# The head of a two-layer backbone: first two chunks modulated one at a time, squares of x summed by TensorE, x ahead of ctx

## The chip, the core and the metric

The kernel runs on one core of one Trainium2 chip. The metric is device time in microseconds (us) of one execution; lower is better. PE is TensorE (matrix products), ACT is ScalarE, DVE is VectorE, SP is SyncE, which here issues all large transfers.

## What is computed

Two layers work on 256 latent tokens (x) and 256 context tokens (ctx) of 2048 channels each. The change lies at the start of layer 0, in the modulated norm and the first part of the input projection:

```
shift_x, scale_x, gate_x = split(silu(c) @ ada_w[0] + ada_b[0], 3)
shift_c, scale_c, gate_c = split(silu(c_ctx) @ ada_w[0] + ada_b[0], 3)
hx = rmsnorm(x, norm_w[0]) * (1 + scale_x) + shift_x
hc = rmsnorm(ctx, norm_w[0]) * (1 + scale_c) + shift_c
q, k, v, ga, u, gb = split(hx @ w_in)        # and the same of hc
```

Everything else (retention, Fourier mixing, gates, output projections, the convolution layer, the final norm) follows it and is written the same in both kernels.

## The kernel before

Channels lie on the 128 partitions and tokens on the free axis. x comes in four tiles xT of 4 channel chunks each (a chunk is 128 channels by 256 tokens, 512 KB a tile), ctx in four tiles cT. Products are made in parts: a weight tile is split into a high part whi (ACT, L95) and the rest wlo (DVE, L59), an activation into a high and a low half of its tile, and three products are summed in PSUM. Products of plain fp32 operands (the sums of squares, gemv) go over PE in two records each.

The head is a sequence of eighths e = 0..7 of 256 channels (two chunks) each.

* `norm_sums` squares the four tiles on ACT (L237, L240; tiles nacc and sq), adds them on DVE (L65), sums over the partitions with two products by a matrix of ones on PE (into pvx for x, pvc for ctx), and takes the root (ACT, L245) and the reciprocal (DVE, L246): rs_x, rs_c.
* `load_ada(e)` loads four tiles (1 MB each) of the modulation weights of one eighth, scale and shift columns of 256 channels. `gemv` multiplies each by the silu of the two conditioning vectors (sc): four products of 512 columns, which use 32 columns of PE each, so four run side by side. `gather` copies the result out of PSUM (gs, L270), `modulation` turns rows into columns with four small products by a selector (gemv<-cols,gs, called row products below) and adds bias and weight on DVE (md), and `mod_stream` makes two modulated chunks of x or of ctx: a DVE step (modt, L196), an ACT step that writes the high half (hx or hc, L197), and a DVE step that writes the low half (L198).
* `main_k` and `main_v` are the dense products of a chunk: q and k of two heads (banks pk and pq), v in pvx, and for ctx k (pk) and v (pvc), with one weight tile w0s[e] per eighth.

In the loop over e the gemv work of eighth e+2 is done between the dense products of eighth e. After eighth 7 ACT makes the silu of a broadcast copy of c (scb) and copies pk, pvx and pvc out of PSUM; then come the projections with streamed weight tiles (gT, gN, gD).

Buffers set who waits: `raw` has 3 slots, which weight tiles w0s and the tiles 0 and 2 of load_ada share in turn; tiles 1 and 3 have a slot each (tags v and scb); whi and wlo have 6. All transfers go through SP in one order. The source fixes which work there is; a scheduler of the language then decides the order of the instructions on each engine, from its own costs, so a change in one place can move rows elsewhere.

```
mds = [prepare(0, load_ada(0))]
mod_stream(0, mds[0], 0)
wraw = load_raw(a["w0s"][0])
load_x(cT, a["ctxT"])
norm_sums(cT, rs_c, pvc[:, 0, :])
mod_stream(0, mds[0], 1)
mds.append(prepare(1, load_ada(1)))
mod_stream(1, mds[1], 0)
mod_stream(1, mds[1], 1)
wn = split_w(wraw, spare)
```

Of the kernel before, what the change touches and what calls it, by code (L numbers as in the profile page):

```python
"""Two-layer hybrid retention / Fourier / short-convolution backbone with a context prefix.

Everything runs in channel-major form (channels on partitions, tokens on the free axis), so
modulation, gates, norms' weights and the convolution are per-partition scalars, and no
activation is ever transposed.  Matrix products are carried by float32r passes: each operand is
split exactly into two 12-bit parts (x = hi + lo) and hi*hi + lo*hi + hi*lo is accumulated in PSUM.
"""
# [13 lines left out]
D = 2048  # L21
# [6 lines left out]
# columns of the packed per-channel vectors  # L28
C_C, C_CC, C_AB0, C_NW0, C_ABG, C_NW1, C_FNW, C_LOG, C_CV, C_SEL = 0, 16, 32, 64, 80, 144, 160, 176, 192, 288
N_COLS = 290  # L30
# columns of the packed shape-only tables
# [4 lines left out]
def body(tc, a, out):  # L36
    nc = tc.nc
    es = ExitStack()
    with es:
# [27 lines left out]
        # ---------------------------------------------------------------- constants  # L67
# [11 lines left out]
        # ---------------------------------------------------------------- weight stream  # L79
# [5 lines left out]
        def split_w(raw, spare=None):  # L85
            """Exact 12-bit parts of a weight tile, by quarters; the last quarter can use spare slots."""
            parts = []
            for pc in range(4):
                sl = raw[:, pc * 512:(pc + 1) * 512]
                if spare and pc == 3:  # L90
                    hi, lo = spare()
                else:
                    hi = wp.tile([P, 512], F32R, tag="whi", bufs=6, name="whi")
                    lo = wp.tile([P, 512], F32R, tag="wlo", bufs=6, name="wlo")
                nc.scalar.copy(hi[:], sl)  # L95
                sub(lo[:], sl, hi[:])
                parts.append((hi, lo))
            return parts
# [6 lines left out]
        def bg():  # L105
            """One background task at every second weight tile."""
            if quiet[0]:
                return
            turn[0] ^= 1
            if tasks and turn[0]:  # L110
                tasks.pop(0)()
# [7 lines left out]
        def group_t(wd, i0, nkt, streams):  # L119
            """Channel-major product of 256 output columns; per stream a pair of banks [hi.W + lo.hi | lo.W]."""  # L120
            ps = [psum("gT") for _ in streams]
            for kt in range(nkt):
                raw = load_raw(wd[i0 + kt])
                bg()
                for pc, (hi, lo) in enumerate(split_w(raw)):
                    for k2 in range(2):
                        kc = kt * 8 + pc * 2 + k2
                        fst, lst = kc == 0, kc == nkt * 8 - 1
                        for t, st in zip(ps, streams):
                            x = st[kc // 2]  # L130
                            for m in range(2):
                                c0 = k2 * 256 + m * 128
                                mm(t[:, m, :], hi[:, c0:c0 + 128], x[:, kc % 2, :], fst, False)
                                mm(t[:, m, 0:256], lo[:, c0:c0 + 128], x[:, kc % 2, 0:256], False, lst)
                    if pc % 2:
                        hook()
            return ps

        def group_d(wd, i0, nkt, x):
            """As group_t for one stream, with all three products summed in place: a bank of two column halves."""  # L140
# [16 lines left out]
        def group_n(wd, i0, streams):  # L157
            """Token-major product of 512 output columns; per stream a pair of banks (token tiles)."""
# [19 lines left out]
        def lr(pool, t, name="t2", bufs=5):  # L178
            """Sum of the two halves of a channel-major bank pair."""
            r = pool.tile([P, 2, 256], F32, tag="t2", bufs=5, name="lr_r")  # L180
            nc.scalar.copy(r[:], t[:, :, 256:512])
            s = pool.tile([P, 2, 256], F32, tag=name, bufs=bufs, name=name)
            add(s[:], t[:, :, 0:256], r[:])
            return s

        def rstd_bc(pool, ps_sum, n):
            """Reciprocal root of the mean plus eps, from sums already broadcast over partitions."""
# [5 lines left out]
        def modulate(pool, dst, x, col, shift, rs):  # L193
            """dst (hi | lo) = x * col * rs + shift."""
# [6 lines left out]
        def split_act(dst, y):  # L201
            """dst[:, m] = (hi | lo) of y[:, m]."""
# [9 lines left out]
        # ---------------------------------------------------------------- start: norms and first modulation  # L212
# [34 lines left out]

        scol = const.tile([P, 32], F32, name="scol")
# [3 lines left out]
        # 1 + scale bias  # L252
# [7 lines left out]
        norm_sums(xT, rs_x, pvx[:, 0, :])  # L260
# [6 lines left out]
        def gather():  # L267
            """Copies the four partial rows out of PSUM."""
# [4 lines left out]
        def modulation(e, gs):  # L273
            """Rows to columns; (scale, shift) of both streams, then the modulated chunks of this eighth."""
# [18 lines left out]
        def main_k(e, k2, w):  # L293
            hi, lo = w
            kc = 2 * e + k2
            for x, blocks in ((hx[e], kq_x), (hc[e], k_c)):
# [7 lines left out]
        def main_v(e, k2, w):  # L304
            hi, lo = w
            kc = 2 * e + k2
            for x, t in ((hx[e], pvx), (hc[e], pvc)):
# [17 lines left out]
        mds = [prepare(0, load_ada(0))]  # L325
        mod_stream(0, mds[0], 0)
        wraw = load_raw(a["w0s"][0])
        load_x(cT, a["ctxT"])
        norm_sums(cT, rs_c, pvc[:, 0, :])
        mod_stream(0, mds[0], 1)  # L330
        mds.append(prepare(1, load_ada(1)))
        mod_stream(1, mds[1], 0)
        mod_stream(1, mds[1], 1)
        wn = split_w(wraw, spare)
        for e in range(8):
# [5 lines left out]
            main_k(e, 0, w[0])  # L341
            if more:
                gemv(raws[0], 0)
            main_v(e, 0, w[1])
# [5 lines left out]
            main_k(e, 1, w[2])  # L350
# [3 lines left out]
            main_v(e, 1, w[3])  # L354
# [8 lines left out]
        # ---------------------------------------------------------------- background: remaining modulation rows  # L363
# [13 lines left out]
        # ---------------------------------------------------------------- retention  # L377
# [3 lines left out]
        # lg: [0:16] = -log gamma, [16:32] = 256 log gamma, [32:48] = log gamma; (forward, backward) x heads  # L381
# [17 lines left out]
        def rope(t, tag, cc, ss):  # L399
            """t [P, 2 heads, 256] (PSUM or SBUF); rotates halves of the partition axis."""  # L400
# [9 lines left out]
        def retention(hh, m, q, k, kc, v):  # L410
            """Stages of one head: scores, weighted values, norm; returns them with the place of the result."""
# [80 lines left out]
        # ---------------------------------------------------------------- Fourier mixing  # L492
        f_es = ExitStack()
        fp = f_es.enter_context(tc.tile_pool(name="fou", bufs=1))
        def table(src, n, name):
            """Splits a table of cosines and sines."""
# [8 lines left out]
        th, tl = table(a["dft"], 512, "t")            # tokens: cos | sin  # L505
        ch, cl = table(a["dftc"], 256, "c")           # channels: cos 0..127 | cos 128, -sin 1..127
        # folded tokens-by-channels operands: even part, odd part (column 0 stays zero), middle channel
# [11 lines left out]
        def fold(pu):  # L519
            """Even and odd parts of u over the channel index, tiles [P, (token half, group), channel]."""  # L520
# [19 lines left out]
        def fourier(g):  # L540
            """Stages of one channel group: the channel tables by its weights, the token transform, their product."""
            got = {}

            def mm3(o, x, y, start, stop):
                """o += x^T y, operands given as (hi, lo)."""
# [86 lines left out]
        # ---------------------------------------------------------------- output projection, layer 0  # L632
        # gv: gate0 | scale1 | shift1 | gate1
# [9 lines left out]
        def project(wd, xs, gcol, xin, acc, first=None, post=None):  # L643
            """x1 = xin + gate * projection; returns its rows' reciprocal root mean square, after which all
            blocks of x1 but the last are scaled by the columns from post on."""
# [5 lines left out]
            for b in range(8):  # L651
# [16 lines left out]
                else:  # L668
# [4 lines left out]
                    # the root's table is in place before it is needed  # L673
# [20 lines left out]
        # ---------------------------------------------------------------- layer 1  # L694
# [46 lines left out]
def _tile_t(w):  # L741
    """[K, 256] -> [K/1024, 128, 2048]: channel-major weight tiles of 8 k-chunks by 256 columns."""
# [4 lines left out]
def _tile_n(w):  # L747
    """[2048, 512] -> [4, 128, 2048]: token-major weight tiles of 4 k-chunks by 512 columns."""
    return w.reshape(4, 4, P, 512).transpose(0, 2, 1, 3).reshape(4, P, 2048)
# [6 lines left out]
def _layout(i):  # L756
# [16 lines left out]
    # scale | shift columns of layer 0, an eighth (256 channels) at a time  # L773
    s = np.stack([ada[0][:, D:2 * D], ada[0][:, 0:D]])            # 2, k, n
    s = s.reshape(2, 4, 4, P, 8, 256).transpose(4, 1, 3, 2, 0, 5)  # e, kq, p, k4, sc/sh, n
    a["ada0"] = s.reshape(32, P, 2048)
# [22 lines left out]
    for b in range(16):  # L799
        for part in (1, 2, 0, 3):                                  # cg, xt, bg, g  # L800
# [4 lines left out]
    # tables of shapes alone  # L805
    j = np.arange(256).reshape(2, P)
    dd = (np.arange(256)[None, None, :] - j[:, :, None]).astype(np.float32)          # i - j
# [4 lines left out]
    cs, sn = np.cos(ang).T.astype(np.float32), np.sin(ang).T.astype(np.float32)      # 64, T  # L812
# [27 lines left out]
```

## Time and profile before

| what | value |
|---|---|
| median of 3 runs | 1834.75 us (1834.25 to 1835.87) |
| span of the profiled execution | 1833.4 us, so the median stands 1.35 us above it |
| busy share of the span | PE 98%, PEld (weight loads) 84%, DVE 66%, ACT 49% |
| first product of eighth 1 starts | 50.18 us |
| last product of eighth 7 starts | 155.40 us |
| read from HBM | 397 MB, 218 GB/s over the span |

The time of the profiled execution itself is not among the three; its span, from the first instruction to the last, is what the lines below belong to. A line of the order of time has the start, the length, the engine, the source line, the operation, what it writes and reads, and in brackets the idle time before it and what ended that. A busy PE is not always a fast one: its granted clock is 1.00 or 0.50, and a view of stretches shows it.

### The profile page before, as it was taken

How to read it: one execution, taken by the hardware profiler on the slowest of the kernel's cores; microseconds unless marked ns; L12 is line 12 of the kernel's file. 1: busy time of each engine (PE TensorE's matmuls, PEld its weight loads, DVE VectorE, ACT ScalarE, POOL GpSimd, SP SyncE). 2: the span in 40 equal slices, each digit the busy share in tenths (PEclk: the TensorE clock that was granted, in tenths of full speed). 3: DMA queues.
4: the chain of work that ended last, by engine and by line, in shares of the span. 5: the costliest groups of instructions: out<-in, count | busy, mean ns of one | idle time of the engine just before them, and what ended most of it. 6: DMA issues, size and time to landing. Idle time of an engine off the chain costs nothing.

```text
span 1833.4 us, 26739 instructions
## 1 busy us (share of the span) xinstructions
PE 1792.8 (98%) x10200; PEld 1541.9 (84%) x10200; DVE 1202.4 (66%) x1862; ACT 906.0 (49%) x1491; POOL 0.2 (0%) x4
## 2 busy tenths in 40 slices
PE   5999999999999999999999999999999999999997
PEld 3667888888888888888978888888888888888887
DVE  5347747557477777777587888666666666665554
ACT  4225626345265554444555555555555555555553
POOL 0000000000000000000000000000000000000000
PEclk8999999999999999999999999999999999999999
DMA  9886445545466676777547877555555555555552
GB/s 389 327 319 246 144 156 184 180 165 186 150 238 250 243 258 229 262 291 287 196 161 253 299 279 288 191 187 197 191 184 191 196 188 185 189 199 186 186 192 105
DMA packets 58449, 400.87 MB, mean 219 GB/s; under 512 B 6480, under 2 KB 6608, under 8 KB 11088
## 3 DMA queue, kind: packets, MB, share of 16 engines
q1 hardware_dynamic: 58320, 399.16, 60.5%
q8 instruction: 80, 1.31, 0.3%
q14 instruction: 49, 0.40, 0.1%
HBM read 397.03 MB, written 2.10 MB: 218 GB/s over the span
## 4 chain that ended last, share of the span: by engine, by line
PE 95%; DVE 2%; ACT 1%; DMA 1%; issue 0%; SPq 0%; DVEq 0%
PE gT L56 70%; PE gN L56 12%; PE gD L56 3%; PE gemv L56 2%; PE pk L56 1%; PE o L56 1%; PE pvc L56 1%; PE pvx L56 1%; PE pP L56 1%; PE S L56 1%; PE pz L56 1%; PE py L56 1%; DMA raw<-w0s 1%; PE pq L56 1%; DMA xT<-xT 0%
## 5 line engine op out<-in xcount | busy, mean ns | idle before, releaser
L95 ACT CAST whi<-raw 128x512 fp32r<-128x512 f32 x1088 | 670.9, 622 | 746.1 <-PE gT L56 535.8
L59 DVE TENSOR_TENSOR wlo<-raw,whi 128x512 fp32r<-128x512 f32 x1088 | 738.3, 690 | 452.4 <-ACT whi L95 436.7
L56 PE MATMUL gT<-h,whi 128*128 128x512 f32 x2048 | 711.3, 392 | 4.2 <-DVE h L198 4.2
L56 PE MATMUL gT<-h,wlo 128*128 128x256 f32 x2048 | 573.2, 280 | 0.0
L56 PEld LDWEIGHTS gT<-h,whi 128*128 128x128 f32 x2048 | 383.6, 187 | 88.8 <-issue 4.5
L56 PEld LDWEIGHTS gT<-h,wlo 128*128 128x128 f32 x2048 | 387.5, 189 | 0.7 <-DVE wlo L59 0.3
L56 PE MATMUL gT<-hx,whi 128*128 128x512 f32 x704 | 254.5, 401 | 1.6 <-ACT v L478 1.6
L56 PE MATMUL gT<-hx,wlo 128*128 128x256 f32 x704 | 197.9, 281 | 0.1
L371 DVE CUSTOM_DVE_ANT_0 raw<-raw,scb 128x2048 f32<-128x2048 f32 x64 | 146.5, 2290 | 48.0 <-DMA raw<-adaT 45.0
L56 PEld LDWEIGHTS gT<-hx,whi 128*128 128x128 f32 x704 | 132.2, 188 | 32.3 <-ACT v L478 2.1
L56 PE MATMUL gT<-y,whi 128*128 128x512 f32 x448 | 155.3, 391 | 0.0
L56 PE MATMUL gN<-whi,hx 128*128 128x512 f32 x448 | 139.3, 392 | 0.0
L56 PEld LDWEIGHTS gT<-hx,wlo 128*128 128x128 f32 x704 | 132.9, 189 | 1.8 <-DVE wlo L59 0.7
L56 PE MATMUL gT<-y,wlo 128*128 128x256 f32 x448 | 125.4, 280 | 0.0
L56 PEld LDWEIGHTS gT<-y,whi 128*128 128x128 f32 x448 | 83.8, 187 | 18.4
L56 PEld LDWEIGHTS gN<-whi,hx 128*128 128x128 f32 x448 | 83.5, 188 | 16.9
L56 PE MATMUL gN<-wlo,hx 128*128 128x512 f32 x224 | 87.3, 390 | 0.0
L56 PEld LDWEIGHTS gT<-y,wlo 128*128 128x128 f32 x448 | 84.7, 189 | 0.0
L56 PE MATMUL gT<-yB,whi 128*128 128x512 f32 x224 | 79.5, 399 | 0.0
L56 PE MATMUL gT<-yA,whi 128*128 128x512 f32 x224 | 79.4, 398 | 0.0
L56 PE MATMUL gT<-yB,wlo 128*128 128x256 f32 x224 | 62.9, 281 | 0.0
L56 PE MATMUL gT<-yA,wlo 128*128 128x256 f32 x224 | 62.9, 281 | 0.0
(233 smaller groups left out, 1792.4 us busy)
## 6 DMA issues: line engine op xcount, KB each, us to landing
raw<-w SPq DMA_DIRECT2D x200, 1024.0 KB, 4.9
raw<-adaT SPq DMA_DIRECT2D x64, 1024.0 KB, 4.9
raw<-ada SPq DMA_DIRECT2D x32, 1024.0 KB, 6.9
raw<-w0o SPq DMA_DIRECT2D x32, 1024.0 KB, 4.9
raw<-w1o SPq DMA_DIRECT2D x32, 1024.0 KB, 4.8
raw<-w0s SPq DMA_DIRECT2D x8, 1024.0 KB, 5.7
xT<-xT SPq DMA_DIRECT2D x4, 512.0 KB, 6.7
cT<-ctxT SPq DMA_DIRECT2D x4, 512.0 KB, 16.2
```

Of the source, the lines that this page charges most:

```text
L56: nc.tensor.matmul(o, l, r, start=start, stop=stop, skip_group_check=True)
L59: nc.vector.tensor_tensor(o, x, hi.bitcast(F32), op=ALU.subtract)
L95: nc.scalar.copy(hi[:], sl)
L371: nc.vector.tensor_tensor_reduce(out=raw[:], in0=raw[:], in1=scb[:], scale=1.0, scalar=0.0, op0=ALU.mult, op1=ALU.add, accum_out=gv[:, j:j ...
```

## The change

Three things are done at the start, the third in two places.

* The squares of x are summed by PE: ACT squares half tiles (128x512, eight of them), and PE multiplies each of the sixteen chunks by the matrix of ones. DVE adds nothing there any more. For ctx `norm_sums` stays.
* Eighth 0 is modulated chunk by chunk: the four tiles of `ada0` of this eighth are packed anew, two for each chunk, with 8 products of 256 columns from each tile, a copy half as wide, and two row products instead of four. `load_first`, `first` and `mod_first` do it.
* The dense products of x of eighth 0 (both chunks) stand ahead of the norm of ctx and of the gemv of eighth 1; those of ctx stay in the loop. The first weight tile is split before ctx is loaded.

Comments and doc strings are dropped, and line numbers move (L270 becomes L282 for `gather`, the copy in `first` is L357).

```diff
+        def norm_sums_pe(tiles, rs, ps):
+            for q in range(4):
+                for h in range(2):
+                    sq = rp.tile([P, 2, 256], F32, tag="t2", bufs=5, name="sq2")
+                    nc.scalar.square(sq[:], tiles[q][:, 2 * h:2 * h + 2, :])
+                    for k in range(2):
+                        i = 4 * q + 2 * h + k
+                        mm(ps[:, 0:256], ones[:], sq[:, k, :], i == 0, i == 15)
+            nc.scalar.activation(rs[:], ps[:, 0:256], AF.Sqrt, bias=eps[:], scale=1.0 / D)
+            nc.vector.reciprocal(rs[:], rs[:])
...
-        norm_sums(xT, rs_x, pvx[:, 0, :])
+        norm_sums_pe(xT, rs_x, pvx[:, 0, :])
...
-        def main_k(e, k2, w):
+        def main_k(e, k2, w, only=(0, 1)):
...
-        mds = [prepare(0, load_ada(0))]
-        mod_stream(0, mds[0], 0)
+        def load_first(k2):
+            got = []
+            for i in range(2):
+                if k2:
+                    raw = (rp.tile([P, 2048], F32, tag="v", bufs=1, name="raw") if i == 0
+                           else wp.tile([P, 2048], F32, tag="scb", bufs=1, name="raw"))
+                    nc.sync.dma_start(raw[:], a["ada0"][2 * k2 + i])
+                else:
+                    raw = load_raw(a["ada0"][2 * k2 + i])
+                got.append(raw)
+            return got
+
+        def first(k2, raws):
+            for i in range(2):
+                for j in range(8):
+                    t = j % 4
+                    mm(gp[32 * t:32 * t + 32, 0:256], sc32[:, i * 8 + j, :], raws[i][:, j * 256:j * 256 + 256],
+                       i == 0 and j < 4, i == 1 and j > 3)
+            gs = rp.tile([P, 512], F32, tag="cst", name="gs")
+            nc.vector.tensor_copy(gs[:, 0:256], gp[:, 0:256])
+            for n in range(2):
+                mm(gp[:, 2 * n:2 * n + 2], gs[:, n * 128:n * 128 + 128], cols[:, C_SEL:C_SEL + 2], True, True)
+            md = rp.tile([P, 4, 2], F32, tag="md", bufs=2, name="md")
+            for n in range(2):
+                c = C_AB0 + 16 * n + k2
+                add(md[:, n, :], gp[:, 2 * n:2 * n + 2], cols[:, c:c + 1].to_broadcast([P, 2]))
+            mul(md[:, 0, :], md[:, 0, :], cols[:, C_NW0 + k2:C_NW0 + k2 + 1].to_broadcast([P, 2]))
+            return md
...
+        r0 = load_first(0)
         wraw = load_raw(a["w0s"][0])
+        r1 = load_first(1)
+        m0 = first(0, r0)
+        mod_first(0, m0, 0)
+        wn = split_w(wraw, spare)
         load_x(cT, a["ctxT"])
+        main_k(0, 0, wn[0], (0,))
+        main_v(0, 0, wn[1], (0,))
+        m1 = first(1, r1)
+        mod_first(1, m1, 0)
+        main_k(0, 1, wn[2], (0,))
+        main_v(0, 1, wn[3], (0,))
+        raws1 = load_ada(1)
         norm_sums(cT, rs_c, pvc[:, 0, :])
-        mod_stream(0, mds[0], 1)
-        mds.append(prepare(1, load_ada(1)))
+        mod_first(0, m0, 1)
+        mod_first(1, m1, 1)
+        mds = [None, prepare(1, raws1)]
         mod_stream(1, mds[1], 0)
         mod_stream(1, mds[1], 1)
-        wn = split_w(wraw, spare)
         for e in range(8):
...
-            main_k(e, 0, w[0])
+            streams = (0, 1) if e else (1,)
+            main_k(e, 0, w[0], streams)
```

How the order moves is shown at three places. The first is the stream of transfers on SP, from the first weight tile on (raw<-w0s) to the second; ada is `ada0`, and L82 is a `raw` slot, L227 and L344 the slots v and scb. Before:

```order
L82 DMA raw<-w0s 128x2048
L218 DMA cT_103<-ctxT 128x1024
L218 DMA cT_104<-ctxT 128x1024
L218 DMA cT_105<-ctxT 128x1024
L218 DMA cT_106<-ctxT 128x1024
L82 DMA raw<-ada 128x2048
L227 DMA raw<-ada 128x2048
L82 DMA raw<-ada 128x2048
L227 DMA raw<-ada 128x2048
L82 DMA raw<-w0s 128x2048
```

The same stretch after, up to the last two tiles of eighth 1:

```order
L82 DMA raw<-w0s 128x2048
L344 DMA raw<-ada 128x2048 x2
L218 DMA cT_103<-ctxT 128x1024
L218 DMA cT_104<-ctxT 128x1024
L218 DMA cT_105<-ctxT 128x1024
L218 DMA cT_106<-ctxT 128x1024
L82 DMA raw<-ada 128x2048 x2
L82 DMA raw<-w0s 128x2048
L227 DMA raw<-ada 128x2048 x2
```

The first weight tile has two tiles of eighth 0 ahead of it instead of four, and the second weight tile has moved between the tiles of eighth 1.

The second place is the end of eighth 0's x products on PE (hx_80 and hc_88 are the modulated tiles of eighth 0) and the norm of ctx on DVE. PE before:

```order
L56 MATMUL pvx<-wlo,hx_80 128x512
L56 MATMUL gemv<-raw,sc_79 32x512 x8
L56 MATMUL pvc<-nacc,ones 128x256 x2
L56 MATMUL pk<-hx_80,whi 128x256 x2
L56 MATMUL pk<-hx_80,wlo 128x256
L56 MATMUL pk<-hx_80,whi 128x256 x2
L56 MATMUL pk<-hx_80,wlo 128x256
L56 MATMUL gemv<-raw,sc_79 32x512 x4
L56 MATMUL pk<-hc_88,whi 128x256
L56 MATMUL pvc<-whi,hc_88 128x512
L56 MATMUL gemv<-raw,sc_79 32x512 x4
```

PE after:

```order
L56 MATMUL pvx<-wlo,hx_80 128x512
L56 MATMUL pvc<-nacc,ones 128x256 x2
L56 MATMUL gemv<-raw,sc_79 32x512 x12
L56 MATMUL pk<-hc_88,whi 128x256
L56 MATMUL pvc<-whi,hc_88 128x512
```

DVE before, from the last sum of ctx's squares on:

```order
L65 TENSOR_TENSOR nacc<-nacc 128x512
L246 RECIPROCAL rs_c<-rs_c 128x256
L196 SCALAR_TENSOR_TENSOR modt<-cT_103,md,rs_c 128x256 x2
L198 SCALAR_TENSOR_TENSOR hc_88<-modt,md,hc_88 128x256 x2
L270 COPY gs<-gemv 128x512
L59 TENSOR_TENSOR wlo<-raw,whi 128x512 x4
```

DVE after:

```order
L65 TENSOR_TENSOR nacc<-nacc 128x512
L59 TENSOR_TENSOR wlo<-raw,whi 128x512 x4
L246 RECIPROCAL rs_c<-rs_c 128x256
L196 SCALAR_TENSOR_TENSOR modt<-cT_103,md,rs_c 128x256 x2
L198 SCALAR_TENSOR_TENSOR hc_88<-modt,md,hc_88 128x256 x2
L282 COPY gs<-gemv 128x512
```

On PE the last three gemv groups of eighth 1 now all stand ahead of the first ctx product; on DVE the split of the second weight tile has moved ahead of the reciprocal of rs_c (on ACT its four casts stand ahead of the root in the same way).

The third place is the passage from eighth 1 to eighth 2 on PE, from the row products on. Before:

```order
L56 MATMUL gemv<-cols,gs 128x2 x4
L56 MATMUL gemv<-raw,sc_79 32x512 x4
L56 MATMUL pk<-hx_82,whi 128x256
L56 MATMUL pq<-hx_82,whi 128x256
L56 MATMUL pvx<-whi,hx_82 128x512
L56 MATMUL gemv<-raw,sc_79 32x512 x4
```

After:

```order
L56 MATMUL gemv<-cols,gs 128x2 x4
L56 MATMUL gemv<-raw,sc_79 32x512 x8
L56 MATMUL pk<-hx_82,whi 128x256
L56 MATMUL pq<-hx_82,whi 128x256
L56 MATMUL pvx<-whi,hx_82 128x512
```

Two groups stand side by side behind the row products. It is so for eighths 2 to 6 after, and was so for 5 and 6 before; the fourth group has moved behind all but a few of the ctx products of each eighth.

More of the change, by code (lines that the diff above doesn't have):

```diff
@@ L291, in mod_stream @@
                          md[:, 2 + k2, s:s + 1], rs)
-        def main_k(e, k2, w):
+        def main_k(e, k2, w, only=(0, 1)):
             hi, lo = w
             kc = 2 * e + k2
-            for x, blocks in ((hx[e], kq_x), (hc[e], k_c)):
+            for x, blocks in [((hx[e], kq_x), (hc[e], k_c))[i] for i in only]:
                 xh, xl = x[:, k2, 0:256], x[:, k2, 256:512]
@@ L302, in main_k, with main_v @@
                     mm(o, lo[:, c0:c0 + 128], xh, False, kc == 15)
-        def main_v(e, k2, w):
+        def main_v(e, k2, w, only=(0, 1)):
             hi, lo = w
             kc = 2 * e + k2
-            for x, t in ((hx[e], pvx), (hc[e], pvc)):
+            for x, t in [((hx[e], pvx), (hc[e], pvc))[i] for i in only]:
                 for m in range(2):
@@ L327, in body, with mod_first @@
+        def mod_first(k2, md, s):
+            dst, src, rs = ((hx, xT, rs_x), (hc, cT, rs_c))[s]
+            modulate(rp, dst[0][:, k2, :], src[0][:, k2, :], md[:, 0, s:s + 1], md[:, 1, s:s + 1], rs)
+        r0 = load_first(0)
         wraw = load_raw(a["w0s"][0])
+        r1 = load_first(1)
+        m0 = first(0, r0)
+        mod_first(0, m0, 0)
+        wn = split_w(wraw, spare)
         load_x(cT, a["ctxT"])
+        main_k(0, 0, wn[0], (0,))
+        main_v(0, 0, wn[1], (0,))
+        m1 = first(1, r1)
@@ L340, in body @@
             raws = load_ada(e + 2) if more else None
-            main_k(e, 0, w[0])
+            streams = (0, 1) if e else (1,)
+            main_k(e, 0, w[0], streams)
             if more:
                 gemv(raws[0], 0)
-            main_v(e, 0, w[1])
+            main_v(e, 0, w[1], streams)
             if e < 7:
@@ L349, in body @@
                 gemv(raws[2], 2)
-            main_k(e, 1, w[2])
+            main_k(e, 1, w[2], streams)
             if more:
@@ L353, in body @@
                 gs = gather()
-            main_v(e, 1, w[3])
+            main_v(e, 1, w[3], streams)
             if more:
@@ L775, in _layout @@
     s = s.reshape(2, 4, 4, P, 8, 256).transpose(4, 1, 3, 2, 0, 5)
-    a["ada0"] = s.reshape(32, P, 2048)
+    s = s.reshape(32, P, 2048)
+    f0 = np.stack([ada[0][:, D:D + 256], ada[0][:, 0:256]]).reshape(2, 2, 8, P, 2, P)
+    s[0:4] = f0.transpose(4, 1, 3, 2, 0, 5).reshape(4, P, 2048)
+    a["ada0"] = s
     g = np.concatenate([ada[0][:, 2 * D:].T, ada[1][:, D:2 * D].T, ada[1][:, 0:D].T, ada[1][:, 2 * D:].T])
```

## The prediction

> **What bounds the kernel now.** I read the page first, for the span and the two bands that matter, TensorE (PE) and the DMA engines.
>
> ```profile
> span 1833.4 us, 26739 instructions
> ...
> PE   5999999999999999999999999999999999999997
> ...
> DMA  9886445545466676777547877555555555555552
> ```
>
> One slice is 46 us. PE is full in all but the first and the last, and the change touches the first three slices. So I went to the view of stretches (columns: stretch, length, busy time of PE, PEld, DVE, ACT, POOL, PE's granted clock, DMA share, GB/s).
>
> ```profile
> 10.00:20.00 10.00, 6.22 (x24) 2.00 (x28) 5.05 (x5) 3.87 (x4) 0.00 (x0) 1.00 1.01 426
> 20.00:30.00 10.00, 6.01 (x32) 3.38 (x25) 6.35 (x14) 5.03 (x9) 0.00 (x0) 0.75 1.02 416
> 30.00:40.00 10.00, 8.71 (x51) 5.10 (x50) 5.56 (x6) 2.69 (x4) 0.00 (x0) 0.91 1.01 421
> 40.00:50.00 10.00, 9.58 (x54) 6.81 (x54) 5.68 (x14) 3.54 (x8) 0.00 (x0) 0.83 1.01 421
> 50.00:60.00 10.00, 10.00 (x70) 7.35 (x67) 2.92 (x7) 3.40 (x7) 0.00 (x0) 1.00 0.79 272
> ```
>
> Until 50 us the DMA engines are full at 416 to 426 GB/s, 2.5 us for a tile of 1 MB, and PE waits; from 50 us on PE is full and the DMA engines are not. What the head is worth is therefore one number: when the first product of the second eighth (hx_81) starts, with all of the first eighth done. The order of time on PE (start, length, engine, line, operation, count, idle before it) gives that, and the work ahead of it:
>
> ```profile
> 15.71 2.07 PE L56 MATMUL pvx<-nacc,ones 128*128 128x256 f32 x4 [0.71 <-DVE nacc L65]
> 17.72 4.67 PE L56 MATMUL gemv<-raw,sc 128*32 128x512 f32 x24
> 23.21 1.05 PE L56 MATMUL gemv<-cols,gs 128*128 128x2 f32 x8 [0.82 <-DVE gs L270]
> 25.78 0.58 PE L56 MATMUL pq<-hx,whi 128*128 128x256 f32 x1 [1.51 <-ACT hx L197]
> ```
>
> ```profile
> 34.02 1.92 PE L56 MATMUL gemv<-raw,sc 128*32 128x512 f32 x16
> 35.87 1.13 PE L56 MATMUL pvc<-nacc,ones 128*128 128x256 f32 x4
> ...
> 40.42 0.39 PE L56 MATMUL pk<-hc,whi 128*128 128x256 f32 x1 [1.71 <-ACT hc L197]
> ...
> 47.50 0.95 PE L56 MATMUL gemv<-cols,gs 128*128 128x2 f32 x8
> ...
> 50.18 0.39 PE L56 MATMUL pk<-hx,whi 128*128 128x256 f32 x1
> ```
>
> Before 25.78 PE has no dense product to do; 47.50 to 50.18 is the chain from the rows of eighth 1 to its first product, 2.7 us.
>
> **The change, part by part.** Prices on the other engines, from the order of time on ACT and DVE:
>
> ```profile
> 5.84 1.06 ACT L237 ACTIVATE nacc<-xT 128x1024 f32<-128x1024 f32 x1 [1.07 <-DMA xT<-xT]
> ...
> 17.83 0.47 ACT L245 ACTIVATE rs_x<-pvx,eps 128x256 f32<-128x256 f32 x1 [2.85 <-PE pvx L56]
> 22.89 2.18 ACT L95 CAST whi<-raw 128x512 fp32r<-128x512 f32 x4 [4.59 <-DMA raw<-w0s]
> ...
> 41.21 2.17 ACT L95 CAST whi<-raw 128x512 fp32r<-128x512 f32 x4 [0.45 <-DMA raw<-w0s]
> ```
>
> ```profile
> 18.33 1.75 DVE L246 RECIPROCAL rs_x<-rs_x 128x256 f32<-128x256 f32 x1 [2.67 <-ACT rs_x L245]
> 22.47 0.69 DVE L270 COPY gs<-gemv 128x512 f32<-128x512 f32 x1 [2.38 <-PE gemv L56]
> ...
> 24.70 0.88 DVE L196 SCALAR_TENSOR_TENSOR modt<-xT,md,rs_x 128x256 f32<-128x256 f32 x2
> 25.50 2.49 DVE L59 TENSOR_TENSOR wlo<-raw,whi 128x512 fp32r<-128x512 f32 x4
> ...
> 28.70 1.22 DVE L65 TENSOR_TENSOR nacc<-nacc,sq 128x1024 f32<-128x1024 f32 x1
> ```
>
> *Landings.* The bytes are the same, their order is not. The first w0s tile lands at 22.9 as the 7th MB (2 of xT, 4 of ada, itself). Now the two tiles of chunk 0 are MB 3 and 4 (15.4), w0s MB 5 (17.9), the tiles of chunk 1 MB 6 and 7 (22.9), ctx as before (27.9). Then SP issues two tiles of eighth 1 (32.9), the second w0s (35.4), and the other two: the last one is MB 14, one later than before, at 40.4 by the rate, or 41.2, when the old MB 14 (the second w0s, cast from 41.21) landed.
>
> *Sum of squares.* Off DVE go three 1024-wide adds and a 512-wide one (about 4.4 us). On ACT 4 squares become 8 of half the size, about 0.6 each. Onto PE come 14 more fp32 products of 256 columns. Two took 2.0 us at half clock (15.71 to 17.72) and, at full, about 0.9 (35.87). From 6.5 (5.84 plus a square) 16 of them end at 20.2 if all are at half clock and at 13.4 if none is. The clock decides, so here are its stretches, cut where it could switch, each 3.41 us:
>
> ```profile
> 14.75:18.16 3.41, 2.70 (x12) 1.38 (x12) 0.88 (x2) 0.56 (x2) 0.00 (x0) 1.00 1.01 425
> 21.58:24.99 3.41, 1.86 (x16) 0.97 (x8) 1.34 (x5) 2.10 (x4) 0.00 (x0) 1.00 1.02 408
> 28.40:31.82 3.42, 3.38 (x11) 2.90 (x12) 2.30 (x3) 1.06 (x1) 0.00 (x0) 0.50 1.01 422
> 38.64:42.06 3.42, 1.71 (x15) 0.56 (x11) 2.43 (x5) 1.75 (x4) 0.00 (x0) 1.00 1.01 417
> 141.03:144.45 3.42, 2.40 (x16) 2.03 (x14) 3.25 (x9) 0.00 (x0) 0.00 (x0) 1.00 0.93 357
> 154.69:158.10 3.41, 1.78 (x8) 1.17 (x7) 3.41 (x8) 3.36 (x6) 0.00 (x0) 1.00 0.92 382
> ```
>
> A stretch that PE fills (28.40) brings the full clock; 79% (14.75) did not. After 54% and 50% (21.58, 38.64) the clock fell to half, while 70% and once 52% (141.03, 154.69) left it full. With the same cuts PE fills 7.9 to 11.3, so the norm ends at 16.0. Root and reciprocal (0.47, 1.75) bring rs_x to 18.3, 1.8 earlier than now.
>
> *Chunk 0.* Its 16 small gemv products cost what 8 wide ones do (1.9 for x16 at 34.02) and end at 17.9. The DVE copy waits for rs_x, is half as wide (between 0.16 of a tiny operation and 0.69; I take 0.4), the row products are half of 1.05, bias and weight 0.4, one modt 0.48, one ACT step 0.5: first products at 20.9 instead of 25.78. The remaining ones need the low part, which on DVE stands behind four weight splits (2.49): 23.2 instead of 28.4. An eighth is priced by main(7), which has no gemv in it:
>
> ```profile
> 145.49 0.39 PE L56 MATMUL pk<-hx,whi 128*128 128x256 f32 x1 [2.06 <-ACT hx L197]
> ```
>
> ```profile
> 157.42 0.50 PE L56 MATMUL gT<-hx,whi 128*128 128x512 f32 x1 [1.63 <-ACT v L478]
> ```
>
> 145.49 to 155.8 (157.42 less its wait) is 10.3 for two chunks of both streams. A chunk of x has 12 products of 256 columns and 6 of 512, one of ctx 6 and 6, so x has 4/7: 2.9 a chunk, ctx 2.2, at full clock. Chunk 0 starts cold, turns full at 25.0 and ends at 26.5.
>
> *Chunk 1.* Its second tile's gemv ends at 27.5. From there it shares DVE and ACT with the squares of ctx: the first add (1.22) ends at 27.8, the copy at 28.2, the row products at 28.8; the second add, ahead of the weight multiply, at 30.2, modt at 30.9; ACT does the last square (1.06, to 31.3) before its step, 31.8; the last add ends at 32.6, the low part at 33.0. PE falls cold in between (28.4 to 31.8 holds 1.5 us of work, 44%), so the rest of chunk 1 ends at 36.5, and ctx's two sums at 37.5.
>
> *What is late next.* rs_c. ACT and DVE now do the second w0s split ahead of it, which waits for the landing at 35.4: four casts and four subtractions end at 38.6, the reciprocal at 40.3, modulated ctx at 41.5 (40.42 now). PE meanwhile waits for the last ada tile (40.4), does its gemv until 41.5, then both ctx chunks, 4.4, to 45.9, and the rows chain of 2.5 to 2.7 brings hx_81 at **48.5**, 1.7 earlier. With the landing at 41.2 it is 0.7 less; if the norm of ctx falls on a cold stretch, another 0.5; if 38.6 to 42.1 (64 to 79% busy) drops the clock as in the run before, 1.7 less; if the norm of x stays cold to its end, 4.2 later at the start, of which some 2.5 arrive here, 0.8 later than now. So the head is worth +0.8 to -1.7, and I take **-1.3**, near the warm end, because the 70% rows stayed full.
>
> The Trainium skill weighs in on this ("TensorE: Matmul & The Clock Gate", Part 1, table of states): it has the clock fall only after an idle window of about 3.4 us. This trace differs, since two windows half full brought the drop; by the rule all dense work after 25 us would run at full clock and the head would give -1.7 with no cold case. The page also says that the window runs free of the kernel's start, so where the cuts fall may differ between executions; no row here shows more than one of them.
>
> *The loop.* The order moves gemv work in eighths 2 to 4: two of the four groups now stand side by side behind the row products, as in the later eighths before.
>
> ```profile
> 79.65:95.64 15.99, 15.54 (x102) 10.38 (x100) 6.89 (x16) 4.00 (x8) 0.00 (x0) 1.00 0.87 336
> 111.61:127.06 15.45, 15.13 (x102) 10.47 (x101) 6.89 (x16) 4.00 (x8) 0.00 (x0) 1.00 0.91 341
> ```
>
> ```profile
> 80.92 1.07 PE L56 MATMUL gemv<-raw,sc 128*32 128x512 f32 x8 [0.32 <-DVE md L65]
> ```
>
> ```profile
> 112.89 1.92 PE L56 MATMUL gemv<-raw,sc 128*32 128x512 f32 x16 [0.32 <-DVE md L65]
> ```
>
> Same work, 15.99 with groups apart and 15.45 with two together: 0.54 each, 1.6 for three, and 0.1 for a pair joined in eighth 1. Against it, the last group moves towards the end of each eighth. The copy that follows needs about 0.9 of cover after it, and two eighths keep three 512-column products, 0.7: 0.4 lost. The row chain into eighth 7 no longer has a weight split in its middle (0.6 of DVE, 0.3 net). The loop: **-1.5**. No transfer holds it: at 336 GB/s with 0.87 busy, the queue has room.
>
> *Hidden at nothing.* Dropping comments, the extra selector rows, and the removed DVE adds (DVE then waits for landings anyway). SP's stream is moved as told; POOL's queue does nothing here. From 158 us the order differs by single rows and PE stood there without gaps.
>
> **Sum.** -1.3 - 1.5 = -2.8 against the execution of 1833.4 us: 1830.6 of span. The median, 1834.75, stands 1.35 above that span, so 1832.0.
>
> **The rivals.** (1) *Warm from 35 us on, landing at the rate*: head -1.8 (a rows chain of 2.5) and loop -1.9 with no cover lost, -3.7, so 1831.0. For it: the 70% rows. Against: the 50% row at 38.64 lies in this very place. The Trainium skill's rule above leads here too. (2) *The head gives nothing*: the last ada tile is one MB later and PE cold behind it, hx_81 at 50, the loop alone, 1833.2. For it: the DMA share of 1.01 until 50 us, since no byte less is moved. Against: PE has 4 us less to do after 40. (3) *Slower, at 145 us*. There ACT turns into the bound, and PE waits for its copy of v:
>
> ```profile
> 148.73 1.92 ACT L366 ACTIVATE scb<-scb 128x2048 f32<-128x2048 f32 x1
> ```
>
> ```profile
> scb<-cb SPq DMA_DIRECT2D x1, 1024.0 KB, 5.6
> ```
>
> The new order issues scb behind one more weight tile, and its slot comes free with the last gemv group, which now stands 2 us nearer to the end. Issued 0.8 us before the row products and 5.6 in flight it lands 0.2 us before ACT wants it. Each tile of 2.5 us that has to go first then delays ACT, the copy and PE alike; two of them cost 4.8, and 1832.0 becomes 1836.8. It decides from 3 us of delay on. Against: one tile is queued there at most, long before.
>
> **How the numbers follow.** 0.2% is 3.7 us, about what a measurement of this kernel can tell from no change: below 1831.1 is faster, above 1838.4 slower. Forecast 0.50 (its own range 1831.1 to 1833.0), rival 1 0.25, rival 2 0.17, rival 3 0.08. Faster: most of rival 1, 0.20, and the low edge of the forecast, 0.07; slower: the half of rival 3 with more than two tiles, 0.04; same 0.69. The range leaves out a tenth on each side, the far part of rival 1 and rival 3: 1829.8 to 1835.2.
>
> **What would show it.** First hx product at 20.9 (not before 22: the norm was cold); the x products in two blocks with a gap between 28 and 32; hc's first product near 41.5; hx_81 at 48.5 (above 50: rival 2); 15.5 us from row products to row products in every eighth; 1.6 us of wait ahead of the first gT product (above 4: rival 3). The forecast is wrong if PE waits anywhere after 60 us for something that it did not wait for before.

## The result, and the profile after

The changed kernel takes 1848.62 us (median of 4 runs, 1848.07 to 1850.3), the kernel before 1834.5 beside it (4 runs, 1833.82 to 1835.87): a ratio of 1.0078, 95% interval 1.0064 to 1.0092. It is 14 us slower, where 1832.0 was forecast. The ratios here and below leave out executions whose mean clock was far lower (two: 1895.4 us at 0.905 for the kernel before, 2227.9 us at 0.75 for the last experiment).

The page of after, its span and the two bands shown of before:

```profile
span 1846.8 us, 26869 instructions
...
PE   7999999999999999999999999999999999999997
...
DMA  9986344544477666687547777555555555555552
```

The first slice is fuller than before. The order of time on PE shows the head and the first product behind the loop:

```profile
19.68 0.51 PE L56 MATMUL pk<-hx,whi 128*128 128x256 f32 x1 [1.51 <-ACT hx L197]
...
30.71 1.93 PE L56 MATMUL gemv<-raw,sc 128*32 128x512 f32 x8 [2.82 <-DMA raw<-ada]
...
41.85 0.39 PE L56 MATMUL pk<-hc,whi 128*128 128x256 f32 x1 [0.23 <-ACT hc L197]
...
48.77 0.39 PE L56 MATMUL pk<-hx,whi 128*128 128x256 f32 x1
```

```profile
154.79 0.50 PE L56 MATMUL gT<-hx,whi 128*128 128x512 f32 x1 [0.79 <-ACT v L535]
```

Eighth 1 starts at 48.77 instead of 50.18, the first gT product at 154.79 instead of 157.42. The gain lasts to the first product of layer 1, of before and then of after:

```profile
930.03 0.76 PE L56 MATMUL gT<-h,whi 128*128 128x512 f32 x1 [4.15 <-DVE h L198]
```

```profile
926.96 0.47 PE L56 MATMUL gT<-h,whi 128*128 128x512 f32 x1 [4.15 <-DVE h L198]
```

There the changed kernel is 3.07 us ahead, and at the end of its span 13.4 behind. So 16.5 us are lost in layer 1: from this product to the first product of the last stage (gD) it takes 867.1 us before and 883.6 after. No wait stands there. The groups of 1000 to 1600 us on PE (count, busy time, mean of one, idle ahead), before and then after:

```profile
L56 PE MATMUL gT<-h,whi 128*128 128x512 f32 x1732 | 600.5, 391 | 0.0
L56 PE MATMUL gT<-h,wlo 128*128 128x256 f32 x1732 | 485.0, 280 | 0.0
```

```profile
L56 PE MATMUL gT<-h,whi 128*128 128x512 f32 x1700 | 600.7, 399 | 0.0
L56 PE MATMUL gT<-h,wlo 128*128 128x256 f32 x1699 | 477.2, 281 | 0.0
```

PE idles for nothing in either and has the full clock in both, but it starts 1732 pairs of one whi and one wlo product in 600 us in the one and 1700 in the other (a product cut by an edge is counted too): 346.7 and 353.3 ns a pair, as the starts give them. The layer has 2,496 such pairs (2,048 with h, 448 with y); by 6.6 ns they are 16.5 us, the whole loss. The order of time shows two rhythms, before and then after (start, length; rows are left out, so that each listing spans three pairs):

```profile
1300.05 0.39 PE L56 MATMUL gT<-h,whi 128*128 128x512 f32 x1
1300.28 0.28 PE L56 MATMUL gT<-h,wlo 128*128 128x256 f32 x1
1300.40 0.39 PE L56 MATMUL gT<-h,whi 128*128 128x512 f32 x1
...
1301.09 0.39 PE L56 MATMUL gT<-h,whi 128*128 128x512 f32 x1
```

```profile
1300.31 0.40 PE L56 MATMUL gT<-h,whi 128*128 128x512 f32 x1
1300.54 0.28 PE L56 MATMUL gT<-h,wlo 128*128 128x256 f32 x1
1300.66 0.40 PE L56 MATMUL gT<-h,whi 128*128 128x512 f32 x1
...
1301.37 0.40 PE L56 MATMUL gT<-h,whi 128*128 128x512 f32 x1
```

The view rounds to 10 ns; in the single ns of the trace, a whi product of the kernel before is followed after 230 ns and a wlo product after 116 or 117, pair after pair. After, the steps go round in three pairs, 236, 232, 240 and 114, 118, 120: 1060 ns for three pairs instead of 1040.

What differs at the start of layer 1 is PE's order. Its first two groups (A and B) overlap there, because the modulated blocks h_4 to h_7 come late. Written short (A4 is group A with h_4, h a whi product, l a wlo product):

```
before: A3 hlhlhlhl B0 h A4 hlhl B0 lhlhlhl B1 h A4 hlhl B1 lhlhlhl A5 hlhl B2 h A5 hlhl B2 lhlhlhl
        B3 hlhlhlhl B4 h A6 hlhlhlhl B4 lhlhl A7 hlhl B4 hl B5 hlhlhl A7 hlhl B5 hl B6 hlhlhlhl ...
after:  A3 hlhlhlhl A4 hlhl B0 h A4 hlhl B0 lhlhlhl B1 h A5 hlhl B1 lhlhlhl B2 h A5 hlhl B2 lhlhlhl
        B3 h A6 hlhl B3 lhlhlhl B4 h A6 hlhl B4 lhlhl A7 hlhl B4 hl A7 hlhl B5 hlhlhlhl B6 ...
```

Two products of one kind follow each other at 8 places before and at 10 after; behind the last of them, some 17 us into the layer, the alternation is unbroken in both. The rotation of buffers differs too: other slots for whi and wlo, other PSUM banks.

### The profile page after: what moved, and what is told of

It is laid out like the page before. It is cut to its first block, busy times and chain, and to the rows that moved or that the text cites. A ratio compares the mean times of both kernels' runs of the same rounds, so it can differ in the third digit from the quotient of the medians.

```text
span 1846.8 us, 26869 instructions
## 1 busy us (share of the span) xinstructions
PE 1814.6 (98%) x10260; PEld 1552.1 (84%) x10260; DVE 1200.2 (65%) x1862; ACT 904.7 (49%) x1495; POOL 0.2 (0%) x4
## 4 chain that ended last, share of the span: by engine, by line
PE 97%; DMA 1%; DVE 1%; ACT 0%; issue 0%; DVEq 0%; SPq 0%; ACTq 0%
PE gT L56 72%; PE gN L56 12%; PE gD L56 2%; PE gemv L56 2%; PE pvx L56 2%; PE o L56 1%; PE pk L56 1%; PE pvc L56 1%; PE pP L56 1%; DMA raw<-ada 1%; PE S L56 1%; PE pq L56 1%; PE pz L56 1%; PE py L56 1%; DMA xT<-xT 0%; DVE fo L62 0%
## 5 line engine op out<-in xcount | busy, mean ns | idle before, releaser
L56 PE MATMUL gT<-h,whi 128*128 128x512 f32 x2048 | 724.9, 399 | 4.2 <-DVE h L198 4.2
```

The source lines that it names most:

```text
L56: nc.tensor.matmul(o, l, r, start=start, stop=stop, skip_group_check=True)
```

## The experiments

Four theories. **A**: the alternating products have more than one steady rhythm; which one holds is left by the last place at which two products of one kind follow each other, and it then lasts. **B**: the rhythm is fixed where the clock comes back to full at the start of layer 1 (at 932.9 us before, 931.1 after). **C**: the addresses of layer 1's parts and banks decide. **D**: the squares' sums on PE do it.

**Parts of the change.** The changed kernel without its first part:

```diff
-        norm_sums_pe(xT, rs_x, pvx[:, 0, :])
+        norm_sums(xT, rs_x, pvx[:, 0, :])
```

> The changed kernel with the squares of x summed by VectorE again, as before; the other two parts stay. PE's order in layer 1 and every address there are those of the changed kernel. Theory A (the rhythm of the alternating whi and wlo products is left by the last place at which two products of one kind follow each other; it then lasts): layer 1 begins as in the changed kernel, so 353.3 ns per pair of products between 960 and 1600 us, and about 1848 to 1850 us. Theory B (the rhythm is fixed where in a product the clock comes back to full at the start of layer 1): the clock falls elsewhere against the products, so 347 or 353 is left to chance. Theory C (the addresses that the rotation of buffers gives to the weights' parts and banks of layer 1): addresses as in the changed kernel, 353.3. Theory D (the sums on PE themselves do it, by what they leave behind): 346.7 and about 1832 us.

And the kernel before with that part alone (the same line the other way round):

> The kernel before with the squares of x summed by PE as the only edit. PE's order in layer 1 and every address there are those of the kernel before. Theory A: 346.7 ns per pair between 1000 and 1600 us; the time within 2 us of the kernel before, since the head ends only a few tenths earlier. Theory B: 347 or 353, left to where the clock comes back. Theory C: 346.7. Theory D: 353.3 and about 1849 us.

They took 1848.63 us (1.0075, 1.006 to 1.009) and 1833.8 (0.9984, 0.9965 to 1.0004). The groups of 1000 to 1600 us, of the first and of the second:

```profile
L56 PE MATMUL gT<-h,whi 128*128 128x512 f32 x1699 | 600.4, 399 | 0.0
```

```profile
L56 PE MATMUL gT<-h,whi 128*128 128x512 f32 x1732 | 600.5, 394 | 0.0
```

D falls; A and C both stand. By its time the first part alone can't be told from no change. The execution of it that was profiled (1831.81 us, the third fastest of ten) is early all the same:

```profile
926.70 0.76 PE L56 MATMUL gT<-h,whi 128*128 128x512 f32 x1 [4.15 <-DVE h L198]
```

That is as early as the changed kernel (926.96), and not the few tenths of the expectation; the changed kernel without its first part comes there at 925.42. So in these traces, one of each, the gains of the parts ahead of layer 1 do not add up.

**The order changed at places in layer 1.** In group_t the wlo products of a quarter are held until pat whi products are out; tn counts layer 1's weight tiles:

```diff
+                    pat = {(16, 0): 2, (32, 0): 4, (48, 0): 2, (64, 0): 2, (64, 2): 2, (80, 0): 4,
+                           (96, 0): 2, (112, 1): 2}.get((tn[0], pc), 1)
...
-                                mm(t[:, m, 0:256], lo[:, c0:c0 + 128], x[:, kc % 2, 0:256], False, lst)
+                                held.append((t[:, m, 0:256], lo[:, c0:c0 + 128], x[:, kc % 2, 0:256], False, lst))
+                                if len(held) == pat:
+                                    while held:
+                                        mm(*held.pop(0))
```

> The changed kernel; in eight quarters of layer 1's 128 weight tiles (tiles 16, 32, 48, 64 twice, 80, 96, 112) two or four whi products go ahead of their wlo products, the same products otherwise. Theory A: the steady spacing can change at each of these places, to 346.7 or to 353.3 ns per pair, and what it has become holds until the next place; the time lies between 1833 and 1850 us, by the share of layer 1 that runs at 346.7. Theory B: no place changes it, the clock stays full there: 353.3 throughout and 1848.6 us. Theory C: 353.3 after each place as ahead of it, since the addresses of the other rows are the same: 1848.6 us.

> The kernel before with the same eight places in layer 1. Theory A: the spacing can change to 353.3 ns per pair at a place and then holds until the next: between 1834 and 1850 us. Theories B and C: 346.7 throughout, 1834.5 us.

They took 1838.84 us (1.0022, 1.0013 to 1.0032) and 1839.42 (1.0026, 1.0016 to 1.0037). The view of stretches for the gT products (busy time and count of PE, clock), cut near the places where the rhythm turned, of the changed kernel with the places, and of the kernel before with them:

```profile
960.00:1100.00 140.00, 140.00 (x794) 1.00 0.76 274
1120.00:1190.00 70.00, 70.00 (x406) 1.00 0.65 230
1210.00:1370.00 160.00, 160.00 (x908) 1.00 0.54 186
1390.00:1600.00 210.00, 210.00 (x1213) 1.00 0.55 191
```

```profile
960.00:1100.00 140.00, 140.00 (x810) 1.00 0.77 279
1120.00:1190.00 70.00, 70.00 (x398) 1.00 0.64 224
1210.00:1370.00 160.00, 160.00 (x908) 1.00 0.54 188
1390.00:1600.00 210.00, 210.00 (x1213) 1.00 0.55 191
```

In the same stretches the changed kernel, at 353.3 ns throughout, has 795, 398, 908 and 1191 products, and the kernel before, at 346.7, has 809, 405, 925 and 1214. So the first kernel with the places goes slow, fast, slow, fast, and the second fast, slow, slow, fast. The rhythm turned at tile 32 (near 1110 us) in both, in opposite directions, at tile 48 (1200) in the one, and at tile 80 (1380) in both; the other places left it. The clock is full throughout and the addresses of the rows between are those of the parent kernel: B and C fall.

**One place.** The same code with {(4, 0): 4} as the table, in the changed kernel and in the kernel before:

> The changed kernel with one quarter of one weight tile of layer 1 (the fifth of 128, near 950 us) reordered: its four whi products, then its four wlo products. Theory A: a place of this form turned 353.3 into 346.7 ns per pair in three of three cases in the runs so far, so 346.7 from 950 us on, which gives the whole loss back: 1848.6 less about 2,450 pairs of 6.7 ns = 16.3 us, 1832 to 1833 us, below the kernel before. Theory B and theory C: 353.3 throughout, 1848.6 us.

> The kernel before with the same quarter of the fifth tile reordered. Theory A: a place of this form turned 346.7 into 353.3 ns per pair in the one case seen; if it does so here, about 16 us slower, 1850 to 1852 us, with nothing else touched; if it leaves the rhythm, 1834.5 us. Theories B and C: 346.7 and 1834.5 us.

1832.06 us (0.9977, 0.9959 to 0.9994) and 1851.4 (1.0086, 1.0071 to 1.0101). The groups of 1000 to 1600 us, first and second:

```profile
L56 PE MATMUL gT<-h,whi 128*128 128x512 f32 x1732 | 600.5, 394 | 0.0
```

```profile
L56 PE MATMUL gT<-h,whi 128*128 128x512 f32 x1699 | 600.4, 399 | 0.0
```

Layer 1 takes 867.4 us in the first and 883.3 in the second. Six products in another order, none added, take the loss away from the one kernel and give it to the other.

**Another order throughout.** The changed kernel with pat = 4 everywhere in the helper:

> The changed kernel with every product of this helper, in both layers, in the order four whi, four wlo. Theory A says that the rhythm belongs to the alternation; with another order there is another steady spacing, of which the one block seen so far (930 ns for four whi, 471 for four wlo) gives 350.3 ns per pair: 2,560 pairs of layer 1 by 3.0 ns less than 353.3 is 7.7 us, so about 1841 us, and no place in layer 1 where the spacing changes. Theories B and C say nothing of it: 1848.6 us.

1840.69 us (1.0031, 1.002 to 1.0042), near the 1841 of A's sum:

```profile
L56 PE MATMUL gT<-h,whi 128*128 128x512 f32 x1712 | 467.3, 394 | 0.0
```

600 us by 1712 are 350.5 ns a pair, so this block order lies between the two rhythms, as A had it. That the total fits so well is in part luck: of the 7.9 us gained over the changed kernel, the traces put 5.2 in layer 1 (7.7 expected), 2.2 in layer 0, which the sum did not hold, and less than 1 elsewhere.

**Without x ahead.** The changed kernel without its third part:

```diff
-        main_k(0, 0, wn[0], (0,))
-        main_v(0, 0, wn[1], (0,))
...
-        main_k(0, 1, wn[2], (0,))
-        main_v(0, 1, wn[3], (0,))
...
-            streams = (0, 1) if e else (1,)
+            streams = (0, 1)
```

> The changed kernel without its third part: the products of x of the first eighth stand beside those of ctx in the loop, as before. The buffers' addresses in layer 1 are turned again, and the first rows of layer 1 stand in a third order (the last two products of one kind next to each other come 108 rows into the layer, in the changed kernel 88 and in the kernel before 88). Theory A: 346.7 or 353.3 ns per pair as this order leaves it, and the time follows: about 1834 or about 1850 us, nothing between. Theory D' (the third part costs the loss by itself, whatever the spacing): 1834 us or less.

1854.68 us (1.0102, 1.0085 to 1.0119). Layer 1 runs at 353.3 (1699 pairs in the same 600 us), and it starts late:

```profile
934.30 0.76 PE L56 MATMUL gT<-h,whi 128*128 128x512 f32 x1 [4.15 <-DVE h L198]
```

That is 4.27 after the kernel before and 7.34 after the changed kernel. "Nothing between" missed these 4 us: I had left the head out of the sum. Against the changed kernel, 5.4 us are lost by the first gT product (160.16 for 154.79) and 2.0 in layer 0 behind it; by the medians the third part is worth 6 us (1854.68 for 1848.62). D' falls.

**Products added.** The changed kernel with products into an unread bank, ahead of the groups at these tiles:

```diff
+                        for kind in {8: 'hl', 24: 'l', 40: 'hl', 56: 'h', 72: 'l', 88: 'l', 104: 'h', 116: 'hl'}.get(tn[0], ''):
```

> The changed kernel with products added ahead of eight of layer 1's groups, into a bank that nothing reads: at tiles 8, 40 and 116 one whi and one wlo product (the alternation goes on, one pair more), at tiles 24, 72 and 88 one wlo product alone (two of a kind next to each other), at 56 and 104 one whi product alone. Theory A: the added pairs at 8, 40 and 116 leave the spacing as they find it, and the single products are where it can change between 353.3 and 346.7 ns per pair; time 1834 to 1850 us. Rival A' (any shift in time resets the rhythm, or it is chance at each group): the pairs change it as often as the single products do. Theories B and C: 353.3 throughout, 1848.6 us plus 1.9 us for the 13 products added, some 1850 us.

1840.3 us (1.0033, 1.0021 to 1.0045); the products added are 11, not the 13 of the expectation. Stretches between the places at tiles 8, 24, 40, 56, 72, 88, 104 and 116, and behind the last:

```profile
980.00:1060.00 80.00, 80.00 (x455) 1.00 0.79 283
1070.00:1150.00 80.00, 80.00 (x454) 1.00 0.77 279
1160.00:1240.00 80.00, 80.00 (x454) 1.00 0.54 186
1250.00:1330.00 80.00, 80.00 (x455) 1.00 0.54 184
1340.00:1420.00 80.00, 80.00 (x463) 1.00 0.55 186
1430.00:1510.00 80.00, 80.00 (x463) 1.00 0.56 192
1520.00:1575.00 55.00, 55.00 (x320) 1.00 0.54 190
1590.00:1640.00 50.00, 50.00 (x291) 1.00 0.55 190
```

It is slow up to tile 72 (near 1336 us) and fast behind it. The three pairs left the rhythm; of the five single products one, a wlo, turned it. So a place with two of a kind can turn the rhythm and need not; a shift in time as such did not (A').

**The best version.** The changed kernel with the one place in layer 1 and one in layer 0's output projection, which runs at the slow rhythm in both kernels:

```diff
+        tn[0] = 100000
         rs1 = project(a["w0o"], ys, 0, reload, acc0, t_out)
...
+                    pat = {(4, 0): 4, (100002, 0): 4}.get((tn[0], pc), 1)
```

> The changed kernel with the one reordered quarter in layer 1's fifth tile, as in the run that gave 1832.06 us, and one more in the output projection of layer 0, in the second weight tile after the first group, near 753 us, where the trace shows 353.3 ns per pair up to 897 us. Theory A: that stage goes to 346.7 from there on, about 400 pairs of 6.7 ns, 2.7 us less: 1829.4 us, if the order that reaches layer 1 then still leaves 346.7 behind the second place; if the place in layer 0 leaves the rhythm as it was, 1832 us. Theories B and C: 1848.6 us.

1829.52 us, 0.9966 of the kernel before (0.9946 to 0.9986). The stretch of the projection, changed kernel and then this one:

```profile
770.00:890.00 120.00, 120.00 (x681) 1.00 0.76 280
```

```profile
770.00:890.00 120.00, 120.00 (x694) 1.00 0.76 278
```

It beats both kernels, by 19 us and by 5.

One regularity goes through these runs. A quarter in the order four whi, four wlo turned the rhythm at every place where it stood among alternating products: eight of eight, six times from 353.3 to 346.7 and twice the other way. A quarter with two whi and two wlo products in turn turned it at one place of twelve.

## Why the prediction was wrong

**The head, -1.3: right for this pair of executions, and in part by luck.** hx_81 was put at 48.5 and came at 48.77, which is -1.4. On the way, the first hx product came at 19.68, not 20.9, as the sums on PE ended at 14.9 and not at 16.0; the gap was at 28 to 30.7 (28 to 32 forecast), hc's first product at 41.85 (41.5), and behind the gap PE was cold, from 30.0 to 36.9, as told. But hx_81 moves between executions of one head. The kernel before with the reordered quarter in layer 1, and the changed kernel with the eight places there, have it at:

```profile
48.41 0.39 PE L56 MATMUL pk<-hx,whi 128*128 128x256 f32 x1
```

```profile
49.56 0.39 PE L56 MATMUL pk<-hx,whi 128*128 128x256 f32 x1
```

Three traces with the head of before have it at 48.41 to 50.18, six with the changed head at 48.45 to 49.56, by the means half a microsecond earlier. The cold stretches lie elsewhere in each of them. (Where a trace holds no switch of the clock yet, the view of stretches reads 1.00 whatever the clock is: it gives 1.00 for 14.75 to 18.16 us before, where four records of 256 columns took 2.07 us (15.71), against 1.13 later (35.87).)

**The loop, -1.5: the right way, and of the right size.** From 50.18 and 157.42 to 48.77 and 154.79 it gained 1.2. The stretches from row products to row products are not all 15.45:

```profile
63.39:78.84 15.45, 15.13 (x101) 10.40 (x101) 6.89 (x17) 3.89 (x8) 0.00 (x0) 1.00 0.98 374
78.84:94.30 15.46, 15.14 (x100) 10.41 (x100) 6.89 (x17) 3.89 (x8) 0.00 (x0) 1.00 0.89 329
94.30:109.96 15.66, 15.34 (x100) 10.41 (x100) 6.89 (x17) 3.89 (x8) 0.00 (x0) 1.00 0.90 334
```

This trace also has PE at half clock from 142.66 to 146.07, which that of before has not. In the changed kernel with one place reordered the clock stays full there, and the loop takes 105.1 us instead of 107.2: 2.1 gained.

The wait ahead of the first gT product is 0.79 instead of 1.6, so rival 3 did not happen. By layer 1 the sum of -2.8 had become -3.07 (-2.9 by the means of three traces of before and four of the changed kernel). With one place reordered, the changed kernel gives 1832.06, the forecast's 1832.0. So the sum came out, and its two terms less well: the head gave less and the loop more.

**What failed** is the step "Hidden at nothing": "From 158 us the order differs by single rows and PE stood there without gaps." Both halves are true, and the conclusion is not. The single rows at the start of layer 1 left PE in another rhythm, at 6.6 ns a pair for 2,496 pairs: +16.5, a term that the sum did not have. For the same reason the last test, that the forecast is wrong if PE waits somewhere new, looked for the wrong thing: PE waits nowhere more and is slower all the same. The page of before had the hint, in two means of one kind of product:

```profile
L56 PE MATMUL gT<-h,whi 128*128 128x512 f32 x2048 | 711.3, 392 | 4.2 <-DVE h L198 4.2
...
L56 PE MATMUL gT<-hx,whi 128*128 128x512 f32 x704 | 254.5, 401 | 1.6 <-ACT v L478 1.6
```

392 and 401 ns for the same shape at the same clock: layer 1 of the kernel before stood at the lucky one of two speeds, and 16 us hung on its staying there. No rival held that, so the chance of slower, 0.04, was far too small. (The mean length alone does not tell the rhythm: the run with the one place in the changed kernel goes at 346.7 with a mean of 394, and the run in blocks of four has 394 at 350.5. The count of starts in a stretch does.) The chance that an order shifted by the compiler changes the rhythm of the long stage deserved a rival of its own.

**Which part moved the rows.** With or without the sums on PE the first rows of layer 1 are the same, in either kernel. They differ from before in the three kernels that hold the split first chunks, and differ once more without x ahead. So the split is what is common to all changed orders; it was not run by itself in the kernel before.

**What stays open**: what in PE keeps the rhythm, and what decides at a place whether it turns (why four of a kind always turned it, and two seldom). A weight load takes 187 to 189 ns in both, and no row shows a wait. Nor is the start wholly fixed: of the 53 runs of the kernel before that stand in these comparisons, 49 took 1833.1 to 1838.0 us and four 1849.0 to 1851.2. That is the size of the slow rhythm with the same program and the same addresses, but none of the four was profiled.

## What to carry to other kernels

Where PE is full for long, count the starts of each product by stage, not only the waits: here one shape had two speeds at one clock, and a stage of 870 us gained or lost 2% by a change ahead of it. Before such a change is judged, see whether the long stage kept its rhythm; reordering a few products at its start put it right here, and a gain of 3 us was kept. A gain of that size in a head that waits for transfers needs several traces: its end moved by 1 to 2 us from execution to execution. Rows that move by single places in a stage without waits are not free.

## What the runs showed of the hardware that I had not expected

PE holds a rhythm over 1,700 pairs and 600 us. At half clock (until 932.9 us in the kernel before) the trace shows but one, 0.43 us from a whi product to the next and 0.21 or 0.22 from a wlo product:

```profile
930.80 0.63 PE L56 MATMUL gT<-h,whi 128*128 128x512 f32 x1
931.23 0.41 PE L56 MATMUL gT<-h,wlo 128*128 128x256 f32 x1
931.45 0.63 PE L56 MATMUL gT<-h,whi 128*128 128x512 f32 x1
```

The Trainium skill ("TensorE: Matmul & The Clock Gate", Back-to-back issue gap) gives, as the gap of an isolated product of N columns, N/1.2 ns for the cold clock, which these rows bear out, and N/2.4 + 2.5 ns for the warm one. By that a pair would take 215.8 + 109.2 = 325 ns, an estimate from the page's figures; the trace has 346.7 or 353.3, and the measurement decides. In the changed kernel the clock also fell once more after a stretch that PE had filled to 56% (length, busy time, count, clock):

```profile
139.25:142.66 3.41, 1.90 (x15) 1.00 0.80 267
142.66:146.07 3.41, 3.41 (x15) 0.50 0.76 271
```
